# Half of an S5 layer's gate products moved from its output stage to its input stage

## The chip, the cores and the metric

The kernel runs on one core of a Trainium2 chip. The metric is the device time of one execution in microseconds (us). The engines of the core have one instruction queue each: TensorE (PE, matrix products; PEld is its weight load), VectorE (DVE), ScalarE (ACT), GpSimd (POOL) and SyncE (SP), which issues most of the DMAs. Before the change, three runs took 1774.8, 1778.39 and 1779.83 us.

## The reference, cut to what matters

The program is two layers of a network over 512 latent and 256 context tokens. The first layer is attention. The second, which the change is in, is a bidirectional S5 state-space layer with a gated output:

```python
u, g = split(h @ w_in, 2)              # 2048 channels each; g is used for the latent tokens only
for direction in (forward, backward):  # 128 groups of 16 channels, 64 complex states in each
    x[t] = lam_bar * x[t-1] + b_bar @ u[t]
    y += real(c @ x[t])
y = gelu(y + d * u)                    # tanh form
ya, yb = split(y @ w_glu + b_glu, 2)
out = ((ya * sigmoid(yb)) * silu(g)) @ w_out
```

The kernel treats eight tokens as one step of the recurrence, so that 512 tokens are 64 steps.

## The kernel before, in words

All large products are done as three PE passes over high and low halves (`mm3`, lines 81 to 83). A weight tile of 128x1024 is loaded by SP into `wraw` (2 buffers), ACT casts it to `whi` and DVE subtracts to get `wlo` (line 65; 3 buffers each). `wnext` (line 1023) keeps up to three such tiles ahead of their use; `wsrc` lists them in the order of use.

The S5 layer has these parts.

- **Input loop**, `for t in range(18)`. `u_tile(t)` makes 128 of the 2048 channels of u, for latent and context tokens (48 matmuls on PE), and stores them. `u_load(t-1)` reads them back in another layout. `s_tile(t-2)` makes from them what is added to the states (line 1134, a block of 32 matmuls), and ACT copies it to the state tiles `ST` (lines 1140 to 1143). After every second `s_tile`, `tree` (lines 1164 to 1169, DVE) folds the context tokens into the start state. After every fourth, a new recurrence begins: `rec.append(recur(...))`. There are four of them, each for 32 groups, of 63 steps each.
- **Recurrence.** One step is four small DVE instructions on 128x64 (lines 1179 to 1182), each but the second dependent on earlier ones. `pull(n)` writes n steps of every recurrence under way into the program. In the loop it stands in three or four places of an iteration (12 steps for t from 6 to 14). The scratch tiles `rt1`, `rt2` have two buffers, so at most two steps are under way.
- **Gates.** `gates` computes silu(g) for 128 channels and 512 tokens: 24 matmuls on PE, a tanh on ACT (line 1218), a multiply on DVE (line 1219), a store by SP (line 1220), then `pull(4)`. There are sixteen. All stand behind the input loop: seven ahead of the first output tile, nine between output tiles.
- **Output tiles**, m from 0 to 15. `y_load(m)` has SP load 512 KB twice (`wo`), 256 KB (`u`) and, for every second m, 1 MB (`toe`). `states(m)` has ACT copy the finished states of tile m (lines 1253, 1254); tiles 4q to 4q+3 need the whole of recurrence q. `y_tile(m)` is 48 matmuls on PE (line 1268) and a DVE copy. After m = 2, 3, 6, 7, 10, 11, 14, 15 `gelu` transposes two tiles on PE (line 1281) and runs for each a chain ACT, DVE, ACT, DVE, ACT, DVE (lines 1285 to 1288, 76, 77) through the scratch tile `t`.
- **GLU.** `glu_mm` is a unit of 24 matmuls against eight of the sixteen GELU outputs. The first eight units in `GLU_ORDER` need outputs 0 to 7 only (tiles 0 to 7). Four units stand between the output tiles, the rest behind them, then the output product.

The order between output tiles is a string; the letter g is a gate, a is a GLU unit:

```python
gates(6, gg)
states(0)
gates(1, gg)
...
        if "gggggggg.g.a.aaa"[m] == "g":
            gates(1, gg)
        elif "gggggggg.g.a.aaa"[m] == "a":
            glu_mm()
```

The order of the program is not yet the order on the chip. When the tile context closes, a planner runs through the program against its own cost model. When an engine is free in that model, it gives it the earliest instruction of the program whose inputs and buffers are ready then. The result is a fixed queue per engine, which the chip follows in order. So an instruction can be planned ahead of an earlier one that was still waiting in the model. Once it is in the queue, everything behind it on that engine waits for it.

Of the kernel before, what the change touches and what calls it, by code (L numbers as in the profile page):

```python
# [9 lines left out]
F32 = mybir.dt.float32  # L10
# [8 lines left out]
P = 128  # L19
# [12 lines left out]
def hybrid_mla_s5(ctx, tc, I, O):  # L32
# [895 lines left out]
    def two(i):  # L928
        return ps2[i % 2].tile([P, 2, 512], F32, name="mm2")
# [52 lines left out]
    def res_load(tt, n):  # L982

        c = slice(512 * n, 512 * n + 512)
        if (n, tt // 4) not in gates0:
            g = gates0[n, tt // 4] = xp.tile([P, 512], F32, name="g", bufs=2)
            sp.dma_start(out=g, in_=gtrow[0][tt // 4:tt // 4 + 1, c].broadcast_to([P, 512]))
        x = xp.tile([P, 512], F32, name="x")
        sp.dma_start(out=x, in_=I["xp"][tt * P:(tt + 1) * P, c])
        return x, gates0[n, tt // 4]  # L990
# [4 lines left out]
    for h in range(HEADS):  # L995
# [4 lines left out]
        if h < 9:  # L1000
            if 2 <= h < 8:
                tt = h - 2
                x, g = res_load(tt, 0)
# [11 lines left out]

    GLU_ORDER = [(m, k, h) for h in range(2) for m in range(4) for k in (1, 0)]
    GLU_ORDER += [(m, k, h) for m in range(4, 16) for k in (1, 0) for h in range(2)]
    wsrc = [I["win1"][m] for m in range(32)]
    wsrc += [I["wglu"][m, k][:, D * h:D * h + D] for m, k, h in GLU_ORDER]
    wsrc += [I["wout1"][m] for m in range(8)]  # L1020
    wq, wdma = [], [sp]
# [1 line left out]
    def wnext():  # L1023
        while wsrc and len(wq) < 3:
            raw = wp.tile([P, D], F32, name="wraw", bufs=2)
            wdma[0].dma_start(out=raw, in_=wsrc.pop(0))
            wh = wp.tile([P, D], F32R, name="whi")
            wl = wp.tile([P, D], F32R, name="wlo")
            split(wh, wl, raw)
            wq.append((wh, wl))  # L1030
        return wq.pop(0)

    def proj1(w, s):
        wh, wl = w
        o = bank()[:, :(TL, TC)[s]]
        for kc in range(KC):
            k = slice(kc * P, (kc + 1) * P)
            mm3(o, wh[:, k], wl[:, k], H1[s][:, 0, kc, :], H1[s][:, 1, kc, :], kc == 0, kc == KC - 1)
        return o
# [52 lines left out]
    def win_chunk(c):  # L1092
        pt = wins[c] = winp.tile([P, 4, 2, P], F32, name="pt", bufs=5)
        sp.dma_start(out=pt, in_=wid[c])
# [15 lines left out]
    def u_tile(m):  # L1110
        w = w_first.pop(0) if w_first else wnext()
        ol = o_first.pop(0) if o_first else proj1(w, 0)
        oc = proj1(w, 1)
        ub = up.tile([P, 8, 96], F32, name="ub", bufs=1)
        act.copy(ub[:, :, 0:64], ol.rearrange("p (i k) -> p i k", k=64))
        act.copy(ub[:, :, 64:96], oc.rearrange("p (i k) -> p i k", k=32))
        act.dma_start(out=ud[m].rearrange("i p k -> p i k"), in_=ub)
        act.dma_start(out=udl[m].rearrange("i p k -> p i k"), in_=ub[:, :, 0:64])

    def u_load(m):  # L1120
        us[m] = up.tile([P, 8, 96], F32, name="u", bufs=3)
        sp.dma_start(out=us[m], in_=ud[m].rearrange("i (c g) k -> (i c) (g k)", g=8))

    def s_tile(m):

        if m % 2 == 0:
            scs[m // 2] = up.tile([P, 2, 16, 32], F32, name="sc")
        sc = scs[m // 2]
        for c in (2 * m, 2 * m + 1):
            wi = wins.pop(c)  # L1130
            o = two(c)
            for q in range(4):
                for r in range(2):
                    pe.matmul(o[:, r, 96 * q:96 * (q + 1)], wi[:, q, r, :], us[m][:, 4 * (c % 2) + q, :],  # L1134
                              start=True, stop=True)
            o = o[:, :, :384].rearrange("p r (q k) -> p r q k", k=96)
            g = slice(4 * c % 32, 4 * c % 32 + 4)
            gc = slice(4 * c % 16, 4 * c % 16 + 4)
            st = ST[c // 8].rearrange("p k r g -> p r g k")
            act.copy(st[lo_, :, g, 1:64], o[lo_, :, :, 0:63])  # L1140
            act.copy(st[up_, :, g, 1:64], o[up_, :, :, 63:0:-1])
            act.copy(sc[lo_, :, gc, :], o[lo_, :, :, 64:96])
            act.copy(sc[up_, :, gc, :], o[up_, :, :, 95:63:-1])
# [10 lines left out]
    def tree(k):  # L1154

        x = scs.pop(k)
        gs = slice(16 * k, 16 * k + 16)
        for l in range(5):
            n = 16 >> l
            a = up.tile([P, 2, 16, n], F32, name=f"tr{l}", bufs=1)  # L1160
            b = up.tile([P, 2, 16, 16], F32, name="trb", bufs=1)[:, :, :, :n]
            lr, li = lam(l, gs, n)
            ev, od = x[:, :, :, 0::2], x[:, :, :, 1::2]
            dve.tensor_tensor(a, ev, lr, op=ALU.mult)
            dve.tensor_tensor(b, ev[:, ::-1], li, op=ALU.mult)
            dve.tensor_tensor(a, a, b, op=ALU.add)
            g = slice(16 * k % 32, 16 * k % 32 + 16)
            dst = a if l < 4 else ST[k // 2][:, 0, :, g].unsqueeze(3)
            dve.tensor_tensor(dst, a, od, op=ALU.add)
            x = a  # L1170

    def recur(q, work):

        st = ST[q]
        lr, li = lam(0, slice(32 * q, 32 * q + 32), 0)
        for k in range(63):
            t1 = work.tile([P, 2, 32], F32, name="rt1", bufs=2)
            t2 = work.tile([P, 2, 32], F32, name="rt2", bufs=2)
            dve.tensor_tensor(t1, st[:, k], lr, op=ALU.mult)
            dve.tensor_tensor(t2, st[:, k, ::-1, :], li, op=ALU.mult)  # L1180
            dve.tensor_tensor(st[:, k + 1], st[:, k + 1], t1, op=ALU.add)
            dve.tensor_tensor(st[:, k + 1], st[:, k + 1], t2, op=ALU.add)
            yield

    rec = []

    def pull(n):
        for _ in range(n):
            for r in list(rec):
                if next(r, 0) == 0:  # L1190
                    rec.remove(r)

    for c in range(2):
        win_chunk(c)
    for t in range(18):
        if 1 <= t <= 16:
            u_load(t - 1)
        if t < 16:
            u_tile(t)
            pull(3)  # L1200
        if t < 15:
            for c in (2 * t + 2, 2 * t + 3):
                win_chunk(c)
                pull(3)
        m = t - 2
        if m >= 0:
            s_tile(m)
            pull(3)
            if m % 2 == 1:
                tree(m // 2)  # L1210
            if m % 4 == 3:
                rec.append(recur(m // 4, stp))

    def gates(n, tile):
        for m in itertools.islice(todo, n):
            o = proj1(wnext(), 0)
            g = tile()[:, :TL]
            act.activation(g, o, AF.Tanh, scale=0.5)
            dve.scalar_tensor_tensor(g, g, 1.0, o, op0=ALU.add, op1=ALU.mult)
            sp.dma_start(out=gd[m], in_=g)  # L1220
            pull(4)
# [2 lines left out]

    def gg():
        return stp.tile([P, TL], F32, name="gg", bufs=2)

    ues.close()
    wines.close()
# [46 lines left out]
    def gelu(n):  # L1276

        o = two(0).rearrange("p a (j e k) -> p (a j) e k", e=2, k=64)
        src = ot.pop(n)
        for j in range(8):  # L1280
            pe.transpose(o[:, j], src[:, j].rearrange("p a x -> p (a x)"), ident)
        for e in range(2):
            y = o[:, :, e, :]
            t = ep.tile([P, 8, 64], F32, name="t", bufs=1)
            act.activation(t, y, AF.Square, scale=0.044715 ** 0.5)
            dve.scalar_tensor_tensor(t, t, 1.0, y, op0=ALU.add, op1=ALU.mult)
            act.activation(t, t, AF.Tanh, scale=0.7978845608028654)
            dve.scalar_tensor_tensor(t, t, 1.0, y, op0=ALU.add, op1=ALU.mult)
            v = 2 * n + e
            h, l = (VV[v // 4][:, v % 4, i] for i in range(2))  # L1290
            half_split(t, *(x.rearrange("p (j k) -> p j k", k=64) for x in (h, l)))
            V[v] = h, l
# [18 lines left out]
    y_load(1)  # L1311
    wdma[0] = sp

    gates(6, gg)
    states(0)
    gates(1, gg)
    for m in range(16):
        y_tile(m)
        if m + 2 < 16:
            y_load(m + 2)  # L1320
        pull(4)
        if m < 15:
            states(m + 1)
        if "gggggggg.g.a.aaa"[m] == "g":
            gates(1, gg)
        elif "gggggggg.g.a.aaa"[m] == "a":
            glu_mm()
        if m % 4 == 2:
            VV.append(stp.tile([P, 4, 2, TL], F32R, name="st"))
        if m % 4 >= 2:  # L1330
            gelu(m // 2 - (m % 2 == 0))
# [10 lines left out]
    while GLU_ORDER:  # L1342
        m, k, h = glu_mm()
        if (k, h) == (0, 1):
            g = work.tile([P, TL], F32, name="g")
            sp.dma_start(out=g, in_=gd[m])
            t = work.tile([P, TL], F32, name="t2")
# [10 lines left out]
    with mkpool(name="f_s", bufs=1, side="right") as work:  # L1358
# [34 lines left out]
        for tt in range(4):  # L1393
# [5 lines left out]
            for n in range(2):  # L1399
                c = slice(512 * n, 512 * n + 512)  # L1400
# [106 lines left out]
```

## Time and profile before

| what | value |
|---|---|
| runs | 1774.8, 1778.39, 1779.83 us |
| profiled execution | 1775.6 us |
| its span (first to last instruction) | 1773.8 us |
| granted TensorE clock, mean | 0.941 of full |
| PE busy | 1573.9 us (89%) |
| DVE busy | 948.8 us (53%) |
| ACT busy | 731.1 us (41%) |
| POOL busy | 657.7 us (37%) |

All times below are counted from the start of the span. Full TensorE clock is 2.4 GHz; a granted clock of 0.78 is the mean of a stretch in which the clock was partly at its lower level, 1.2 GHz. Busy times over the whole span say little here: the attention layer, the input loop, the output tiles and the GLU have different limits, so each stretch is read on its own. The input loop lies between about 960 and 1151 us, the output tiles between 1181 and 1336 us, the GLU and the output product behind them.

### The profile page before, as it was taken

Reading aid. Unit: us, or ns where it says so; the run is one execution under the profiler, and the core shown is the slowest. Engines: PE = TensorE matmul, PEld = TensorE weight load, DVE = VectorE, ACT = ScalarE, POOL = GpSimd, SP = SyncE. Lnnn points to the kernel's source line nnn. Section 1 sums busy time; section 2 is a strip of 40 time slices with the busy share of each in tenths; the row PEclk is TensorE's granted clock in tenths of the full one; section 3 lists DMA queues with packets and bytes.
Section 4 is the critical chain, followed back from the end, with each engine's and each line's share of the span. In section 5 each row is a group of like instructions: output and inputs, shape, how many; then the busy total and the mean of one; then the engine's idle time right before and its main releaser. Section 6 shows DMA issues by size and latency. Waiting matters only on the chain.

```text
span 1773.8 us, 26950 instructions
## 1 busy us (share of the span) xinstructions
PE 1573.9 (89%) x9870; PEld 1313.6 (74%) x9870; DVE 948.8 (53%) x2478; ACT 731.1 (41%) x1253; POOL 657.7 (37%) x705
## 2 busy tenths in 40 slices
PE   7548788999887977789999999999869999999997
PEld 4435467887786867678887999988658888888876
DVE  7352222376565755667435288899953433333336
ACT  2221122365545644556214666767473222222220
POOL 2999758899677878771000000000000000000022
PEclk9868798999989988989999999999889999999999
DMA  9216776564455565555424866578462333333442
GB/s 338 75 50 217 240 238 194 161 208 121 143 176 163 169 166 166 164 166 172 125 77 134 258 214 230 171 270 320 154 243 77 123 109 108 108 107 107 128 156 72
DMA packets 157132, 293.60 MB, mean 166 GB/s; under 512 B 55068, under 2 KB 86856, under 8 KB 155976
## 3 DMA queue, kind: packets, MB, share of 16 engines
q1 hardware_dynamic: 122056, 279.07, 48.6%
q10 hardware_dynamic: 34880, 12.78, 2.8%
q8 instruction: 78, 1.28, 0.3%
q14 instruction: 54, 0.44, 0.1%
q0 software_dynamic: 64, 0.03, 0.0%
HBM read 230.39 MB, written 69.55 MB: 169 GB/s over the span
## 4 chain that ended last, share of the span: by engine, by line
PE 53%; DMA 18%; POOL 16%; DVE 5%; issue 4%; ACT 3%; SPq 0%; ACTq 0%; POOLq 0%
PE mm L81 15%; PE mm L83 15%; PE mm L82 15%; DMA wo<-pind 8%; DMA wid<-wo 4%; PE mm L1134 3%; DMA pair<-in_w_mod_dram 2%; DMA wraw<-in_wout_dram 2%; POOL wo L395 1%; POOL pw L393 1%; PE mm L1268 1%; POOL wt L391 1%; POOL bk L361 1%; POOL wo L394 1%; POOL wt L390 1%
## 5 line engine op out<-in xcount | busy, mean ns | idle before, releaser
L65 DVE TENSOR_TENSOR wlo<-wraw,whi 128x1024 fp32r<-128x1024 f32 (+1 forms) x155 | 178.5, 1153 | 337.0 <-ACT whi L65 332.7
L1371 POOL TENSOR_TENSOR x<-x,row_g 128x1024 f32<-128x1024 f32 x4 | 11.3, 2846 | 926.0 <-DMA wraw<-in_wout_dram 886.6
L65 ACT CAST whi<-wraw 128x1024 fp32r<-128x1024 f32 (+1 forms) x155 | 149.4, 965 | 401.3 <-PE mm L82 268.2
L81 PE MATMUL mm<-st,whi 128*128 128x512 f32 x512 | 204.2, 399 | 5.2 <-ACT st L76 5.1
L83 PE MATMUL mm<-st,wlo 128*128 128x512 f32 x512 | 202.5, 396 | 0.0
L82 PE MATMUL mm<-st,whi 128*128 128x512 f32 x512 | 201.4, 393 | 0.8 <-DVE st L77 0.8
L81 PE MATMUL mm<-h,whi 128*128 128x512 f32 (+1 forms) x384 | 138.7, 362 | 0.2 <-DVE bnmv L917 0.2
L82 PE MATMUL mm<-h,whi 128*128 128x512 f32 (+1 forms) x384 | 137.1, 358 | 0.8 <-DVE h L1077 0.8
L83 PE MATMUL mm<-h,wlo 128*128 128x512 f32 (+1 forms) x384 | 136.5, 356 | 0.0
L81 PEld LDWEIGHTS mm<-st,whi 128*128 128x128 f32 x512 | 97.5, 190 | 26.8 <-ACT st L76 6.3
L81 PE MATMUL mm<-hh,whi 128*128 128x512 f32 (+1 forms) x320 | 112.2, 361 | 3.2 <-DVE hh L599 3.2
L82 PEld LDWEIGHTS mm<-st,whi 128*128 128x128 f32 x512 | 97.3, 190 | 23.3 <-DVE st L77 1.6
L83 PEld LDWEIGHTS mm<-st,wlo 128*128 128x128 f32 x512 | 97.4, 190 | 22.6
L83 PE MATMUL mm<-hh,wlo 128*128 128x512 f32 (+1 forms) x320 | 109.7, 346 | 1.1 <-DVE wlo L65 1.0
L82 PE MATMUL mm<-hl,whi 128*128 128x512 f32 (+1 forms) x320 | 110.4, 347 | 0.0
L65 DVE TENSOR_TENSOR ptl<-tr,pth 128x384 fp32r<-128x384 f32 (+1 forms) x160 | 79.0, 524 | 17.3 <-ACT pth L65 16.5
L65 ACT CAST pth<-tr 128x384 fp32r<-128x384 f32 (+1 forms) x160 | 68.5, 462 | 45.9 <-PE tr L832 45.3
L808 ACT ACTIVATE p<-sc,mx 128x768 f32<-128x768 f32 (+1 forms) x96 | 73.6, 766 | 27.9 <-DVE mx L807 27.6
L807 DVE TENSOR_REDUCE mx<-sc 128x1 f32<-128x768 f32 (+1 forms) x96 | 73.8, 772 | 17.4 <-PE sc L797 16.4
L81 PEld LDWEIGHTS mm<-h,whi 128*128 128x128 f32 x384 | 72.9, 190 | 12.0 <-issue 0.5
L82 PEld LDWEIGHTS mm<-h,whi 128*128 128x128 f32 x384 | 73.0, 190 | 10.8 <-DVE h L1077 1.1
L83 PEld LDWEIGHTS mm<-h,wlo 128*128 128x128 f32 x384 | 72.9, 190 | 10.4
(371 smaller groups left out, 4196.5 us busy)
## 6 DMA issues: line engine op xcount, KB each, us to landing
wraw<-in_wglu_dram SPq DMA_DIRECT2D x64, 512.0 KB
wraw<-in_win_dram SPq DMA_DIRECT2D x52, 512.0 KB
wod<-wo SPq DMA_DIRECT2D x32, 512.0 KB
wo<-pind SPq DMA_DIRECT2D x32, 512.0 KB
pw<-in_Bc_dram SPq DMA_DIRECT2D x32, 512.0 KB
wid<-wo SPq DMA_DIRECT2D x32, 512.0 KB
pt<-wid SPq DMA_DIRECT2D x32, 512.0 KB
wo<-wod SPq DMA_DIRECT2D x32, 512.0 KB
```

The costliest lines, as they stand in the source:

```text
L65: return act.copy(hi, src).ins, (eng or dve).tensor_tensor(lo, src, f(hi), op=ALU.subtract).ins
L81: pe.matmul(ps, lh, rh, start=first, stop=False)
L82: pe.matmul(ps, lh, rl, start=False, stop=False)
L83: pe.matmul(ps, ll, rh, start=False, stop=last)
L361: pool.tensor_tensor(bk[rows, :, :, 16 * d:16 * d + 16], b1[rows], b2[rows], op=ALU.add)
L390: eng.tensor_tensor(t1, pr, br, op=ALU.mult)
L391: eng.tensor_tensor(t2, pi, bi, op=ALU.mult)
L393: eng.tensor_tensor(bi, pr, bi, op=ALU.mult)
L394: eng.tensor_tensor(pr, t1, t2, op=ALU.add)
L807: dve.reduce_max(mx[:, 1:2], s, axis=AX.X, negate=True)
L808: act.activation(p[:, a:b], s, AF.Exp, bias=mx[:, 1:2], scale=1.0, accum_out=mx[:, 2:3])
L1134: pe.matmul(o[:, r, 96 * q:96 * (q + 1)], wi[:, q, r, :], us[m][:, 4 * (c % 2) + q, :], start=True, stop=True)
```

## The change

Eight of the sixteen gates are called inside the input loop, behind `u_tile(t)` for t = 4, 5, 7, 8, 10, 11, 13, 14, each with its `pull(4)`. One stays ahead of `states(0)` and one behind it. Six are left between the output tiles, behind m = 0, 2, 4, 6, 8 and 10. The GLU units keep their places. The weight list follows the new order. The scratch tile `t` of the GELU gets a second buffer. `gates`, `todo` and `gg` move up unchanged.

```diff
-    wsrc = [I["win1"][m] for m in range(32)]
+
+    GATE_AT = (4, 5, 7, 8, 10, 11, 13, 14)
+    wsrc = [I["win1"][m] for t in range(16) for m in (t,) + ((16 + GATE_AT.index(t),) if t in GATE_AT else ())]
+    wsrc += [I["win1"][m] for m in range(24, 32)]
...
         if t < 16:
             u_tile(t)
             pull(3)
+            if t in GATE_AT:
+                gates(1, gg)
...
-            t = ep.tile([P, 8, 64], F32, name="t", bufs=1)
+            t = ep.tile([P, 8, 64], F32, name="t", bufs=2)
...
-    gates(6, gg)
+    gates(1, gg)
     states(0)
     gates(1, gg)
...
-        if "gggggggg.g.a.aaa"[m] == "g":
+        if "g.g.g.g.g.ga.aaa"[m] == "g":
             gates(1, gg)
-        elif "gggggggg.g.a.aaa"[m] == "a":
+        elif "g.g.g.g.g.ga.aaa"[m] == "a":
             glu_mm()
```

## Rows read from the trace of the kernel before

**Rows 1.** Engines by stretch: length, busy us (instructions), granted clock, DMA share, GB/s.

```profile
1029.00:1160.00 131.00, 131.00 (x858) 119.27 (x857) 112.28 (x549) 89.94 (x127) 0.00 (x0) 1.00 0.60 198
1160.00:1257.00 97.00, 96.60 (x722) 80.32 (x721) 93.00 (x443) 62.71 (x60) 0.00 (x0) 1.00 0.85 310
1257.00:1280.00 23.00, 16.82 (x63) 11.92 (x63) 22.93 (x121) 7.08 (x11) 0.00 (x0) 0.78 0.35 114
1280.00:1336.00 56.00, 38.94 (x424) 33.05 (x422) 31.47 (x116) 42.69 (x32) 0.00 (x0) 0.85 0.53 193
1360.00:1700.00 340.00, 339.75 (x1485) 278.61 (x1485) 112.45 (x111) 85.03 (x96) 9.80 (x4) 1.00 0.36 117
```

**Rows 2.** Line 1179 alone, by stretch: one instruction is one step of a recurrence.

```profile
1029.00:1160.00 131.00, 23.87 (x108) 1.00 0.60 198
1160.00:1257.00 97.00, 20.62 (x94) 1.00 0.85 310
1257.00:1279.30 22.30, 5.58 (x26) 0.77 0.36 118
1279.30:1315.00 35.70, 5.38 (x24) 0.81 0.59 221
```

**Rows 3.** ACT in order of time: start, us; the copies that wait for a recurrence.

```profile
1279.28 2.07 ACT L1253 COPY sm<-st 64x1024 f32<-64x1024 f32 x1 [4.92 <-DVE st L1182]
...
1314.84 2.08 ACT L1253 COPY sm<-st 64x1024 f32<-64x1024 f32 x1 [1.69 <-DVE st L1182]
```

**Rows 4.** PE in order of time: two matmuls of consecutive gates, 24 matmuls apart.

```profile
1160.08 0.39 PE L82 MATMUL mm<-h,whi 128*128 128x512 f32 x1
...
1165.52 0.39 PE L82 MATMUL mm<-h,whi 128*128 128x512 f32 x1
```

**Rows 5.** Groups of DVE instructions, 1029.2 to 1314.8: busy us, mean ns, idle before.

```profile
L65 DVE TENSOR_TENSOR wlo<-wraw,whi 128x1024 fp32r<-128x1024 f32 x27 | 32.9, 1219 | 6.8 <-ACT whi L65 6.6
...
L1219 DVE SCALAR_TENSOR_TENSOR gg<-gg,mm 128x512 f32<-128x512 f32 x16 | 10.9, 680 | 0.5 <-ACT gg L1218 0.5
```

**Rows 6.** DVE in order of time: starts of steps, one recurrence, then a pair.

```profile
1079.00 0.22 DVE L1179 TENSOR_TENSOR rt<-st,lamt 128x64 f32<-128x64 f32 x1
1079.80 0.22 DVE L1179 TENSOR_TENSOR rt<-st,lamt 128x64 f32<-128x64 f32 x1
...
1087.26 0.23 DVE L1179 TENSOR_TENSOR rt<-st,lamt 128x64 f32<-128x64 f32 x1
...
1088.35 0.22 DVE L1179 TENSOR_TENSOR rt<-st,lamt 128x64 f32<-128x64 f32 x1
```

**Rows 7.** Waits of DVE: us, times, longest; in the loop, then from 1160 to 1315.

```profile
DVE tr L1164 <- ACT sc L1143: 13.7, 6, 3.0
...
DVE st L77 <- ACT st L76: 2.1, 1, 2.1
```

**Rows 8.** SP's own waits, 960 to 1340 us.

```profile
SPq L1094 <- PE mm L1134: 90.8, 20, 8.7
...
SPq L1220 <- DVE rt L1180: 2.5, 4, 0.9
```

**Rows 9.** Chain that ended last: one output tile on PE, one GELU's transposes.

```profile
1189.99 2.77 PE mm L1268 x48
...
1206.86 0.87 PE mm L1281 x8
```

**Rows 10.** Groups of PE instructions, 1257 to 1336: output tiles, GLU units, transposes.

```profile
L1268 PE MATMUL mm<-wo,sm 128*64 128x128 f32 x256 | 22.2, 301 | 7.9 <-ACT sm L1254 7.9
L1268 PE MATMUL mm<-toe,u 128*64 128x128 f32 x120 | 13.5, 306 | 9.1 <-DMA u<-udl 8.8 <-DVE st L1181 0.3
L82 PE MATMUL mm<-st,whi 128*128 128x512 f32 x24 | 12.0, 499 | 0.8 <-DVE st L77 0.8
...
L1281 PE MATMUL mm<-ident,ot 128*128 128x128 f32 x32 | 4.8, 300 | 0.4 <-DVE st L1182 0.4
```

**Rows 11.** DMA rate while output tiles are loaded fastest (columns as in Rows 1).

```profile
1180.00:1200.00 20.00, 19.60 (x179) 16.29 (x179) 18.34 (x99) 13.02 (x10) 0.00 (x0) 1.00 1.02 401
```

More of the change, by code (lines that the diff above doesn't have):

```diff
@@ L1191, in pull, with gates, gg @@
                     rec.remove(r)
+    def gates(n, tile):
+        for m in itertools.islice(todo, n):
+            o = proj1(wnext(), 0)
+            g = tile()[:, :TL]
+            act.activation(g, o, AF.Tanh, scale=0.5)
+            dve.scalar_tensor_tensor(g, g, 1.0, o, op0=ALU.add, op1=ALU.mult)
+            sp.dma_start(out=gd[m], in_=g)
+            pull(4)
+    todo = iter(range(16))
+    def gg():
+        return stp.tile([P, TL], F32, name="gg", bufs=2)
     for c in range(2):
@@ L1212, in hybrid_mla_s5 @@
                 rec.append(recur(m // 4, stp))
[L1214 to L1221, printed above, removed]
-    todo = iter(range(16))
-    def gg():
-        return stp.tile([P, TL], F32, name="gg", bufs=2)
     ues.close()
```

## The prediction

> **What bounds the kernel now.** The busy times by stretch come first, because the change lies between 960 and 1336 us only. In the input loop PE is busy for all of its 131 us at full clock; DVE is busy for 112.3 of them [rows 1]. From 1160 to 1257 both are nearly full. From 1257 to 1336 PE falls behind: it is busy 55.8 of 79 us at a granted clock of 0.78 and 0.85. From 1360 on it is full again, so what is lost before 1336 reaches the end one for one.
>
> What does PE wait for there? The count of steps answers. Of 252 steps 108 are done by 1160, 94 follow by 1257, 26 by 1279, 24 by 1315 [rows 2]. The program places 150 in the input loop (12 per iteration from t = 6 to 14, then 6, 3 and 3 for what is under way). So DVE is some 40 steps behind when the loop ends. ACT copies the states of tile 8 at 1279.28 and those of tile 12 at 1314.84, each time as soon as the recurrence lets it [rows 3]. These are the ends of the third and the fourth recurrence; tiles 8 to 11 and 12 to 15 follow them.
>
> So the gates that the change moves are PE work in a stretch where PE has no gap, and they go to one where it has none either. The eight gates cost 8 x 5.44 = 43.5 us of PE there [rows 4], and the same is taken away behind. PE runs out of other work at about 1257 in both versions, if nothing else intervenes. What decides is when the recurrences end, and what PE has to do meanwhile.
>
> PE's loss now: in 1257 to 1336 it does 72 GLU matmuls at 5.44/24 us (16.3; three units), 376 matmuls of output tiles, 2.77 us for 48 (21.7), and 32 transposes at 0.87 for 8 (3.5) [rows 4, 9, 10]. That is 41.5 us of work in 79 us: 23.2 idle and 14.3 to the lower clock.
>
> **The change part by part.**
>
> *Start of the first recurrence.* It needs the states of `s_tile(3)`, in iteration 5. Two gates now stand ahead of it, at t = 4 and 5, on a PE that has no gap: +10.9 us. DVE has no steps to do in that time, since none is ready. The bounds are 0 (the planner puts these gates behind) and 10.9; I take 10.9, as a ready gate is earlier in the program.
>
> *DVE work done before that start.* Each gate takes a `wlo` of 1.22 and a multiply of 0.68 on DVE [rows 5]. Two gates' worth leaves the later queue: -3.8. The other six are on DVE between the first and the last step before and after: 0.
>
> *Fewer pairs.* A lone recurrence takes 0.79 us a step, two together 1.09 for two steps [rows 6], so a pair saves 0.49. By counting pulls, the old program has 15 pairs of the first two recurrences, 15 of the next two and 39 of the last two: 69. The new one pulls 16 in an iteration with a gate, ends recurrences earlier against the next one's start, and has 7 + 3 + 35 = 45. The 24 lost pairs cost 24 x 0.49 = 11.8 if nothing else fills the gaps of a lone chain, and 0 if tree and split instructions fill all. In the loop they alternate with the steps about half of the time; I take 5.
>
> *Idle DVE in the longer loop.* DVE idles 131 - 112.3 = 18.7 us of the loop, 14%, of which 13.7 stand in front of a tree head that waits for ACT [rows 1, 7], with steps queued behind it. Six gates behind the start lengthen the stretch by 32.6 us; at 14% that is +4.7. The far end is that the longer loop lets the steps into the idle time: -18.7, the third rival. I take the row's own share.
>
> *Second scratch tile.* The two chains of one GELU may now overlap. DVE waited 2.1 us on this chain between 1160 and 1315 [rows 7], so -2.1 at most for the steps queued behind it, which I take; PE's own waits for these outputs fall into the wait for the third recurrence, which covers them. Without that cover the tile would be worth what PE waits for line 77 there, 0.8 us [rows 10], and a little more.
>
> *Stores and waits.* Eight gate stores move on SP ahead of loads for the loop. In the rows such a store waits 0.9 us at longest, while the loop's own loads wait 8.7 for PE to free a buffer [rows 8]; 8 x 0.9 = 7.2 is the far end, 0 the value, the cover being those waits. Behind a store stand the `pt` and `u` loads and the next weight tile. The tanh stands in ACT's queue ahead of the state copies; ACT is busy 89.9 of 131 us [rows 1], so a gate's cast and tanh fit into its 5.44 us. The far end is a further tree head per gate pushed back, already in the idle share.
>
> *Tile loads.* A tile loads 1.84 MB (512 KB twice, 256 KB, and half of 1 MB), a gate 0.52 MB of weights and 0.26 MB stored. Before, a tile with its gate and half a GELU takes 2.77 + 5.44 + 0.44 = 8.65 us of PE for 2.62 MB, 303 GB/s. Now every second of tiles 0 to 7 has a gate: 5.93 us for 2.23 MB, 376 GB/s. The fastest stretch shows 401 GB/s [rows 11], so it just fits: 0. If only 303 to 310 were kept up, a tile would take 7.3 us: 8 x 1.4 = +11 on PE. The Trainium skill, page "Perfetto Trace Analysis", section "Roofline", puts the ceiling of a single core at about 435 GB/s, set by its 16 DMA engines; no run here shows that rate. By it a tile would need 5.1 us, and by the row 5.6; either is under 5.93, and by the page alone the second rival would have less than the chance that I give it.
>
> *Sum for the recurrences.* 10.9 - 3.8 + 5 + 4.7 - 2.1 = +14.7: the fourth ends at about 1329 in place of 1314.8, the third ends 28 lone steps ahead of it in place of 24, which at 35.7/24 us each [rows 2] is 1288.
>
> *What of it reaches PE.* Tiles 12 to 15 follow as before, so the output stage ends 14.7 later. Against that, PE can put GLU units into the longer wait. Eight need only tiles 0 to 7; three were done by 1336, five are left (27 us). Bounds 0 and -14.7. The old order took a unit only where no output tile was ready, and each needs its `wlo` from the same full DVE. I take one unit, -5.4. That leaves +9.3.
>
> 1775.6 + 9.3 = 1784.9 us for an execution like the profiled one, which lies 2.8 under the median of the three runs; against that median it would be 1787.7. I say 1786.
>
> **The rivals.**
>
> *Second: the loads hold the tiles and nothing fills the wait.* Tiles 0 to 7 come late at 376 GB/s, so do their GELUs, and the GLU units can't start while PE waits. Then 14.7 stays whole, and the clock falls with the longer gaps: 14.3 us were lost beside 23.2 idle, so 0.62 x 14.7 = 9.1 more. 1775.6 + 23.8 = 1799.4. For it: the demand is 94% of the best rate shown. Against: the gates can run ahead of the tiles and space them out.
>
> *Third, the other side: the longer loop empties DVE's backlog.* At tree heads DVE stands still with steps in its queue. If the planner puts the steps pulled behind the gates ahead of these heads, the idle 18.7 us are used: 10.9 - 3.8 + 5 - 2.1 - 18.7 = -8.7, or 1766.9; with another GLU unit in a gap 1761.5. It decides from 10.0 of the 18.7 us on. For it: a backlog of 40 steps at the loop's end. Against: the queue is fixed, and before there was as much to place and the gaps stayed.
>
> *Fourth: no net change.* PE has the same work and five GLU units to hide behind: if it takes three in place of one, 9.3 falls to -1.6 or so and the time is 1774 to 1779. The same would show if the planner left the gates where they ran before; with PE full in the loop and the gates ready, little speaks for that.
>
> **How the numbers follow.** Chances: forecast (+2 to +16) 0.42, second 0.14, third 0.27, fourth 0.17. Differences under 0.3%, 5.3 us, can't be told from none. Slower takes 0.35 of the forecast and the second, 0.49. Same takes 0.07 of the forecast and 0.16 of the fourth, 0.23. Faster takes the third and 0.01 of the fourth, 0.28. The forecast's own range is 1778 to 1794. The whole range goes from 1764, under the third case, to 1804, the second case on the median's basis (1802.2) and a little: about 0.1 is left out on each side.
>
> **What would show it.** The first step starts at about 1040 in place of 1029, PE stays full to the end of the loop, and fewer than 154 steps are done when it ends. ACT's first copy for tile 8 comes near 1288 and for tile 12 near 1329, each released by line 1182. DVE's idle time in the loop is 22 us or more. From about 1257 PE waits with a granted clock under 1. I am wrong if the fourth recurrence ends at 1315 or before, if PE has more than four GLU units done when tile 15 is, or if the first recurrence starts as early as before.

## The result and the profile after

The changed kernel takes 1800.4 us (median of four runs, 1794.0 to 1804.5). The kernel before takes 1778.9 beside it. The ratio is 1.0121, with a 95% interval from 1.0095 to 1.0147: slower by 21.5 us. The prediction said 1786, slower, with a range from 1764 to 1804. The profiled span is 1799.1 us, 25.3 more than before. One execution further below stands apart, the profiled one of e5: it took 2218.7 us at a granted clock of 0.648, so it is left out and no row of e5 is read.

The busy times of the changed kernel by stretch, with the columns of [rows 1]:

```profile
960.00:1197.70 237.70, 237.70 (x1487) 213.75 (x1485) 161.56 (x680) 137.20 (x194) 0.00 (x0) 1.00 0.65 205
1197.70:1217.00 19.30, 0.13 (x3) 0.16 (x4) 18.29 (x92) 11.47 (x9) 0.00 (x0) 0.57 0.61 215
1217.00:1303.00 86.00, 79.17 (x620) 65.99 (x620) 77.35 (x370) 49.80 (x50) 0.00 (x0) 0.92 0.72 259
1303.00:1362.00 59.00, 38.46 (x416) 33.72 (x418) 35.26 (x135) 42.19 (x32) 0.00 (x0) 0.80 0.52 183
1362.00:1725.00 363.00, 363.00 (x1598) 298.04 (x1594) 123.93 (x126) 94.25 (x108) 9.48 (x4) 1.00 0.35 115
```

PE is full up to the end of the input loop, now at 1197.7, and full again from 1362 on. Between them lie two stretches of loss. One was there before, at the end of the output tiles. The other is new: 19 us at the loop's end in which PE does nothing. The one PE row that shows it, in order of time:

```profile
1216.88 0.70 PE L1273 MATMUL mm<-toe,u 128*64 128x128 f32 x4 [19.17 <-DMA u<-udl]
```

The steps of the recurrences by stretch (line 1182 in this kernel; compare [rows 2]):

```profile
1029.00:1160.00 131.00, 21.54 (x96) 1.00 0.64 203
1160.00:1257.00 97.00, 19.18 (x86) 0.88 0.66 234
1257.00:1303.00 46.00, 9.54 (x42) 0.91 0.61 212
1303.00:1343.00 40.00, 6.28 (x28) 0.79 0.57 210
```

By 1160 there are 96 steps done (108 before), by 1257 there are 182 (202 before). The ACT copies that need the third and the fourth recurrence, which [rows 3] has at 1279.28 and 1314.84, come 23.8 and 28.2 us later:

```profile
1303.05 2.03 ACT L1258 COPY sm<-st 64x1024 f32<-64x1024 f32 x1
...
1343.03 2.00 ACT L1258 COPY sm<-st 64x1024 f32<-64x1024 f32 x1 [1.69 <-DVE st L1185]
```

The output tiles end at 1362.4 (1336 before, +26.4), and the rest of the program follows at full clock. So the time is lost before 1362, and the question is what on DVE made the fourth recurrence 28 us late. Its groups of instructions between the first step and tile 12's copy (1040.2 to 1343) are: busy us, mean ns, idle time before them.

```profile
L1182 DVE TENSOR_TENSOR rt<-st,lamt 128x64 f32<-128x64 f32 x252 | 56.5, 224 | 4.3
...
L1185 DVE TENSOR_TENSOR st<-st,rt 128x64 f32<-128x64 f32 x252 | 53.5, 225 | 4.3
...
L65 DVE TENSOR_TENSOR wlo<-wraw,whi 128x1024 fp32r<-128x1024 f32 x26 | 31.8, 1224 | 7.5 <-ACT whi L65 7.4
...
L1201 DVE SCALAR_TENSOR_TENSOR gg<-gg,mm 128x512 f32<-128x512 f32 x14 | 9.6, 684 | 0.0
L1276 DVE COPY ot<-mm 128x512 f32<-128x512 f32 x12 | 8.3, 688 | 3.8 <-PE mm L1273 3.7
...
L1293 DVE SCALAR_TENSOR_TENSOR t<-t,mm 128x512 f32<-128x512 f32 x12 | 8.2, 686 | 3.2 <-ACT t L1292 3.1
```

In the kernel before, the same groups between its first step and its tile 12 (1029.2 to 1314.8) that [rows 5] does not show:

```profile
L1179 DVE TENSOR_TENSOR rt<-st,lamt 128x64 f32<-128x64 f32 x252 | 55.4, 220 | 2.9
...
L1182 DVE TENSOR_TENSOR st<-st,rt 128x64 f32<-128x64 f32 x252 | 50.6, 220 | 2.5
...
L1271 DVE COPY ot<-mm 128x512 f32<-128x512 f32 x12 | 8.2, 685 | 0.7 <-PE mm L1268 0.7
...
L1288 DVE SCALAR_TENSOR_TENSOR t<-t,mm 128x512 f32<-128x512 f32 x12 | 8.2, 683 | 0.1
```

The instructions of a step overlap within a line and between lines, so the busy times of the lines don't add up to time on DVE. The step instructions, as the only ones that use the scratch tiles `rt`, can be taken together, and beside them everything on DVE (the third busy time, as in [rows 1]); before, then after:

```profile
1029.20:1314.80 285.60, 164.70 (x1008) 0.96 0.66 233
1040.20:1343.00 302.80, 173.90 (x1008) 0.92 0.64 216
...
1029.20:1314.80 285.60, 266.85 (x1862) 230.12 (x1861) 255.25 (x1219) 183.65 (x215) 0.00 (x0) 0.96 0.66 233
1040.20:1343.00 302.80, 262.49 (x1826) 228.72 (x1824) 261.83 (x1216) 179.78 (x212) 0.00 (x0) 0.92 0.64 216
```

The same 1008 step instructions take 173.9 us in place of 164.7. Counted in the traces in order of time, two recurrences take a step side by side 69 times before and 45 times after, just as the prediction had counted from the pulls. So 24 pairs less go with 9.2 us more, 0.38 each. Idle time grows too, at the output copies (0.7 to 3.8) and in the GELU chain (0.1 to 3.2): these instructions stand in DVE's fixed queue with steps behind them. Over the whole stretch DVE is busy 261.8 us in place of 255.3 and idle 41.0 in place of 30.3. With the later start (1040.2 in place of 1029.2) that is 11.0 + 6.5 + 10.7 = 28.2.

### The profile page after: what moved, and what is told of

The parts are those of the page before. It is cut to its first block, busy times and chain, and to the rows that moved or that the text cites. A ratio compares the mean times of both kernels' runs of the same rounds, so it can differ in the third digit from the quotient of the medians.

```text
span 1799.1 us, 26939 instructions
## 1 busy us (share of the span) xinstructions
PE 1576.0 (88%) x9870; PEld 1319.0 (73%) x9870; DVE 962.2 (53%) x2478; ACT 730.3 (41%) x1253; POOL 659.3 (37%) x705
## 4 chain that ended last, share of the span: by engine, by line
PE 52%; DMA 18%; POOL 16%; DVE 5%; issue 4%; ACT 4%; SPq 1%; ACTq 0%; POOLq 0%; DVEq 0%
PE mm L81 15%; PE mm L82 15%; PE mm L83 15%; DMA wo<-pind 7%; DMA wid<-wo 3%; PE mm L1137 3%; DMA pair<-in_w_mod_dram 2%; DMA wraw<-in_wout_dram 2%; PE mm L1273 1%; POOL wo L394 1%; POOL wo L395 1%; POOL pw L393 1%; POOL wt L390 1%; POOL wt L391 1%; ACT sm L1259 1%
```

## The experiments

Theory A is the prediction's: the fourth recurrence's end sets the end of the output tiles. Theory B is the new hole of 19 us. The table has where the last instruction of each run's last step begins, when ACT copies for tile 12, and the ratio to the kernel before.

| kernel | last step instruction, us | tile 12's copy | span | ratio (95%) |
|---|---|---|---|---|
| before | 1314.6 | 1314.8 | 1773.8 | 1 |
| after | 1342.8 | 1343.0 | 1799.1 | 1.0121 (1.0095 to 1.0147) |
| e1, hole filled | 1345.7 | 1347.3 | 1803.6 | 1.0157 (1.0135 to 1.0179) |
| e2, gates late | 1337.3 | 1337.6 | 1794.1 | 1.0121 (1.0100 to 1.0142) |
| e3, two early gates | 1325.4 | 1326.0 | 1784.5 | 1.0039 (1.0024 to 1.0053) |
| e4, one scratch tile | 1339.1 | 1339.4 | 1798.4 | 1.0113 (1.0092 to 1.0134) |
| e10, no pulls in the loop | 1330.6 | 1330.8 | 1787.8 | 1.0082 (1.0060 to 1.0105) |
| e12, e2 and e10 together | 1319.3 | 1323.9 | 1780.9 | 1.0058 (1.0040 to 1.0075) |
| e11, less on DVE, gates as before | 1307.9 | 1308.5 | 1770.8 | 0.9975 (0.9959 to 0.9991) |

**e1, the hole filled.**

```diff
-    gates(1, gg)
+    gates(6, gg)
...
-        if "g.g.g.g.g.ga.aaa"[m] == "g":
+        if "g..........a.aaa"[m] == "g":
```

> The changed kernel, but with its eight remaining gates arranged as six ahead of the first state copy, one behind it and one behind output tile 0, so that seven stand ahead of the first output tile as before the change. Theory A (the fourth recurrence ends late and sets the end of the output tiles): the 19.2 us in which PE stands idle ahead of the first output tile go away, but the fourth recurrence still ends at 1338 to 1345 us and the time stays at 1796 to 1802 us; PE's idle time comes back ahead of tile 8. Theory B (that idle stretch of 19.2 us is what the change costs): the time falls by 15 to 19 us, to 1781 to 1785 us.

PE is busy for all of 1197.7 to 1217, so the hole is gone, and the time is 1805.6, not less (3.6 above theory A's range). The fourth recurrence ended at 1346, its copy followed at 1347, and PE waited for it there. Theory B as the cost by itself falls: PE had only moved its waiting.

**e2, the gates later in the loop; e3, only two early gates; e4, one scratch tile.** e2:

```diff
-    GATE_AT = (4, 5, 7, 8, 10, 11, 13, 14)
+    GATE_AT = (7, 8, 10, 11, 12, 13, 14, 15)
```

> The changed kernel with its eight loop gates at t = 7, 8, 10, 11, 12, 13, 14, 15, so that none stands ahead of the first recurrence. Theory A: the first step starts at 1029 in place of 1040 us, the fourth recurrence ends 8 to 11 us earlier (1332 to 1335), and the time is 1789 to 1792 us. Theory B: the two gates ahead of the first output tile are as many as before, so the idle stretch and the time stay: 1799 to 1801 us.

e3, against the kernel before (which keeps its string of gates):

```diff
+    GATE_AT = (4, 5)
...
+            if t in GATE_AT:
+                gates(1, gg)
...
-    gates(6, gg)
+    gates(4, gg)
```

> The kernel before with only two gates moved, to t = 4 and 5 (four are left ahead of the first state copy, one scratch tile for the GELU, the order between output tiles as before). Theory A: the first step starts at 1040 us, the fourth recurrence ends 7 to 11 us later (1322 to 1326) and the time is 1786 to 1790 us against 1779. Theory B: with five gates ahead of the first output tile PE has next to no idle stretch there: 1779 to 1782 us.

e4:

```diff
-            t = ep.tile([P, 8, 64], F32, name="t", bufs=2)
+            t = ep.tile([P, 8, 64], F32, name="t", bufs=1)
```

> The changed kernel with one scratch tile for the GELU. Theory A as predicted: the second tile is worth 2 us to the steps queued behind, so 1800 to 1803 us. Theory B: nothing, 1799 to 1801 us. A third view, that two overlapping GELU chains push the steps of the recurrence back in VectorE's queue, gives less than 1797 us.

e3 came as theory A has it: 1785.7 us, tile 12's copy 11.2 later. But in e2, where the first step is back at 1029.2, the copy is only 5.4 earlier than in the changed kernel, the span 5.0 less, and the ratio is the same: 1798.9 us against an expected 1789 to 1792, a miss. The step instructions of e2 and all of its DVE from its first step to tile 12's copy:

```profile
1029.20:1337.60 308.40, 175.82 (x1008) 0.94 0.64 216
...
1029.20:1337.60 308.40, 268.71 (x1874) 233.82 (x1872) 266.62 (x1220) 184.24 (x218) 0.00 (x0) 0.94 0.64 216
```

Of the 11.0 us of earlier start 4.8 go to more busy time than in the changed kernel and 0.8 to more idle time. Two gates' work on DVE stands behind the first step again, and only 39 pairs are left in e2's trace, six fewer than in the changed kernel. So the late start is a real cost, but moving the gates late brings other costs back. e4 (1797.5 us, in none of its three ranges) shows no difference from the changed kernel by its interval; the second scratch tile is worth nothing that can be told.

**e5 and e6, half the steps in every recurrence.** For e5 in the kernel before and for e6 in the changed one:

```diff
-        for k in range(63):
+        for k in range(31):
```

> The kernel before, with every recurrence doing 31 of its 63 steps (the other 32 are left out, so the states behind them are not the reference's). Theory A (the late end of the fourth recurrence sets the end of the output tiles): 128 steps less, some 100 us of DVE, so no recurrence ends last any more; PE's loss between 1257 and 1336 (23.2 us idle and 14.3 from the lower clock) goes: 1738 to 1748 us. Rival C (loads of the output tiles and weight tiles set the pace there, the recurrences only stand beside them): 1760 to 1776, with PE's waits for y tiles put down to DMA.

> The changed kernel with the same 31 steps in every recurrence. Theory A: what the change cost through the recurrences (tile 12's copy 28 us later) is gone; only the wait of 19.2 us ahead of the first output tile, which the recurrences covered, can show now: 1740 to 1765, at most 20 above the shortened kernel before, and after that wait PE has no idle above 5 us before tile 15. Rival C (the loads of the moved gates and of the closer output tiles cost the time): some 21 us or more above the shortened kernel before, spread over the output tiles, PE's waits put down to wo, u or toe.

e5 took 1748.5 to 1754.3 us, ratio 0.9845 (0.9809 to 0.9881). That lies between theory A's range and rival C's. e6 took 1774.5, ratio 0.9971 (0.9953 to 0.9989). Between them lies 0.9971 / 0.9845 = 1.0128, as much as the change costs with full recurrences. Theory A allowed 20 us for the uncovered hole; 21 to 22 came, which is rival C's number. The waits are not spread over loads as rival C has it, though. PE's waits in e6 from 1190 to 1345 (us, times, longest):

```profile
PE mm L1273 <- DMA u<-udl: 17.2, 2, 16.9
PE mm L1286 <- DVE t L1293: 10.6, 5, 2.9
```

No line of a recurrence is in it. So with the recurrences out of the way there is a second limit, by which the change costs as much as by the first: the hole, and waits on the GELU chain behind it.

**e7 and e8, the low halves of the weights on POOL.** For the kernel before (e7) and the changed one (e8):

```diff
             wl = wp.tile([P, D], F32R, name="wlo")
-            split(wh, wl, raw)
+            split(wh, wl, raw, pool)
```

> The kernel before, with the low halves of the S5 layer's weight tiles computed on POOL, which is idle there, in place of DVE. Theory A: the recurrences lose 27 instructions of 1.22 us and 6.8 us of waits for them from DVE's queue (39.7 us); the fourth ends at 1275 to 1295 in place of 1314.8 and PE's loss shrinks as much: 1745 to 1765 us. Rival D: a 128x1024 on POOL takes some 2.8 us (its adds of that size in the last stage) and DVE's small instructions get slower beside it, so weights come later to PE and the recurrences gain under 10 us: 1770 to 1790.

> The changed kernel with the same low halves on POOL. Theory A: 26 instructions of 1.22 us and 7.5 us of waits (39 us) leave DVE's queue, the fourth recurrence ends at 1300 to 1320 in place of 1343.0: 1762 to 1782 us, still above the kernel before with POOL, by 10 to 22, since the recurrences still start 11 us later and are alone more often. If the change's loss were in PE's or the loads' part, the two POOL versions would differ by the same 21 us or more and the wait ahead of the first output tile would set it. Rival D: 1790 to 1810.

e7 took 1798.7 us, ratio 1.0111 (1.0081 to 1.0141): rival D's direction, and past its range. e8 took 1816.2, ratio 1.0212 (1.0177 to 1.0247), past rival D's range too. DVE has 27 instructions less in e7 and its recurrences still end 8 us later than before. Its rows in order of time, POOL and DVE together, show why:

```profile
1040.83 2.45 POOL L65 TENSOR_TENSOR wlo<-wraw,whi 128x1024 fp32r<-128x1024 f32 x1 [9.59 <-ACT whi L65]
1040.83 0.23 DVE L1182 TENSOR_TENSOR st<-st,rt 128x64 f32<-128x64 f32 x1
1041.09 2.26 DVE L1179 TENSOR_TENSOR rt<-st,lamt 128x64 f32<-128x64 f32 x1
1043.28 0.21 DVE L1180 TENSOR_TENSOR rt<-st,lamt 128x64 f32<-128x64 f32 x1
```

A DVE instruction of 0.22 us that comes up while POOL works lasts 2.26 us, until POOL is done. So 1.22 us of DVE's own work was exchanged for some 2.1 us of standing still. More is lost than the recurrences show: e7's output tiles end at 1355.6, 19.5 us late, with PE waiting 11.6 and 9.7 us for DVE ahead of two blocks of transposes, and later 5.1 us for one `wlo` from POOL. The two runs differ by 17.5 us, within theory A's 10 to 22. But since DVE was slowed in both, and neither recurrence ended where theory A had it, the pair does not tell the theories apart.

**e9, the hole filled and half the steps.** The edits of e1 and e6 together:

> The changed kernel with seven gates ahead of the first output tile (none behind tiles 1 to 10 but the one at m = 0), and 31 of 63 steps in every recurrence (the other 32 left out). Theory E (two limits of about the same size, one behind the other: the recurrences end 28 us later, and PE has a hole of 17 to 19 us with waits on the GELU chains behind it; taking away one leaves the other): with both taken away the time is that of the shortened kernel before, 1753 us: 1748 to 1760. Theory A alone would have had the shortened changed kernel there already. Rival C (the moved gates' loads and stores cost the time wherever the gaps are): 1768 us or more, as with the hole.

1774.6 us, ratio 0.9984 (0.9968 to 0.9999), the same as e6: theory E in its simple form, that the hole is the second limit, falls, and rival C's number came. e9 by stretch:

```profile
1198.00:1227.60 29.60, 29.60 (x134) 24.25 (x132) 24.17 (x92) 19.48 (x20) 0.00 (x0) 1.00 0.73 253
1227.60:1260.00 32.40, 24.03 (x277) 20.53 (x277) 26.50 (x104) 24.14 (x19) 0.00 (x0) 0.89 0.96 363
1260.00:1300.00 40.00, 29.07 (x287) 22.35 (x285) 14.64 (x22) 30.56 (x27) 0.00 (x0) 0.82 0.73 260
1300.00:1337.00 37.00, 34.94 (x362) 28.53 (x360) 16.47 (x23) 31.27 (x28) 0.00 (x0) 0.96 0.60 208
```

With the gates spent ahead of the first tile, the tiles and GELUs behind it have no PE work beside them, and PE, bare of gates, loses what the hole had cost. PE's largest wait from 1190 to 1345, and its only one for a load:

```profile
PE mm L81 <- ACT st L76: 17.8, 4, 7.1
...
PE mm L1273 <- DMA wo<-wod: 0.2, 1, 0.2
```

The first is GLU units that wait for a GELU output. So the second limit is the pace of the output stage behind a loop that ends 44 us later (its last s_tile ends at 1195.4 in the changed kernel, 1151.6 before), not the hole as such. For 32 us the DMA engines are nearly full (0.96), but PE hardly waits for them, and of the chain that ended last there one weight tile's load (6.0 us at 1231) is the longest on DMA. So rival C's number came, and its cause is not seen. The trace points at ACT: from 1227.6 to 1337 it is busy 86.0 of 109.4 us, and in that chain the GELU's activations stand behind the copies of `states`, here behind four of them (8.3 us):

```profile
1239.00 2.04 ACT sm L1258
1241.05 2.07 ACT sm L1259
1243.14 2.08 ACT sm L1258
1245.22 2.05 ACT sm L1259
1247.30 0.61 ACT t L1290
```

No run takes these copies off ACT, so this is read from the trace and not shown by an experiment.

**e10, no steps written behind the gates in the loop.**

```diff
-            pull(4)
+            pull(0 if t < 17 else 4)
```

> The changed kernel with no steps written behind the eight gates in the input loop, so that it has the pulls of the kernel before there, and 69 pairs in place of 45. Pair theory (lone steps cost DVE the 7 us more that its step instructions are busy in the changed kernel): step instructions busy 211 to 214 us in place of 218, the fourth recurrence ends 4 to 8 us before 1343, time 1791 to 1797. Rival F (a later place in the program only delays steps, since DVE takes what is ready): the fourth recurrence at 1345 or later, 1800 us or more.

1790.1 us, just under the range. The two lines of a step in e10 that have idle time in front of them, from 1042 to 1331, then its step instructions together and all of its DVE:

```profile
L1182 DVE TENSOR_TENSOR rt<-st,lamt 128x64 f32<-128x64 f32 x252 | 55.8, 222 | 2.7
...
L1185 DVE TENSOR_TENSOR st<-st,rt 128x64 f32<-128x64 f32 x252 | 50.9, 222 | 2.8
...
1042.30:1330.80 288.50, 165.48 (x1008) 0.96 0.66 226
...
1042.30:1330.80 288.50, 254.59 (x1826) 222.03 (x1824) 253.43 (x1217) 179.57 (x212) 0.00 (x0) 0.96 0.66 226
```

The trace has 69 pairs again. The step instructions take 165.5 us, close to the 164.7 before the change, with 5.5 us of idle time in front of them in place of 8.6. The recurrences end 12.2 us earlier (4 to 8 expected): DVE is busy 8.4 us less, which is what the pairs give back (173.9 to 165.5), and idle 5.9 us less, with a first step 2.2 us later. So the pair theory holds for the busy time. That the idle time shrinks as well was not in it, and no run parts the two. Steps that the change put into the program earlier made the end later.

**e12, late gates without pulls.** The edits of e2 and e10 together:

> The changed kernel with its eight gates in the input loop from t = 7 on (so that the first recurrence starts at 1029 again) and no steps written behind them (so that the 69 pairs are back): the two terms of the recurrence path that the runs so far showed one by one (5.4 and 12.2 us at the end of the fourth) are both taken away. If they add, the fourth recurrence ends at 1323 to 1328 (1343.0 in the changed kernel, 1314.8 before) and the time is 1781 to 1788 us. What is left over the kernel before then belongs to neither: the fourth recurrence starts 43 us later, behind a longer loop, and the output stage has the hole ahead of its first tile. If the rest were nothing, the time would be 1779 or less; if the two terms were one and the same, 1789 or more.

1787.5 us, and 1780.9 in the profiled span. The last step's last instruction begins at 1319.3, 23.5 us before that of the changed kernel, and 4.7 behind the kernel before. That is more than the 17.6 of the two terms: with 68 pairs in its trace, e12 also gets back those that e2 had lost. Together the two edits give back most of the 28.2 us. But tile 12's copy does not follow at once, as e12's ACT shows in order of time:

```profile
1322.39 1.04 ACT L65 CAST whi<-wraw 128x1024 fp32r<-128x1024 f32 x1 [3.96 <-PE mm L82]
1323.35 0.62 ACT L1292 ACTIVATE t<-t 128x512 f32<-128x512 f32 x1
1323.88 2.01 ACT L1258 COPY sm<-st 64x1024 f32<-64x1024 f32 x1
```

A weight cast waits 4 us for PE to free its buffer, and the copy is queued behind it. Of the 21.5 us some 11 went (1800.4 - 1787.5 = 12.9 by the medians, 0.0063 of 1778 = 11.2 by the ratios); 10 stay with the recurrences almost back in place. In the profiled execution 7.1 us of span stay, and tile 12's copy is 9.1 late: 4.7 by the recurrence and 4.4 in ACT's queue. The hole is still there too (18.0 us). Whether this is the limit of e6 and e9 is not shown.

**e11, less on DVE, the gates as before.** Against the kernel before:

```diff
+            act.copy(sc[lo_, :, gc, :], o[lo_, :, :, 64:96])
+            act.copy(sc[up_, :, gc, :], o[up_, :, :, 95:63:-1])
             act.copy(st[lo_, :, g, 1:64], o[lo_, :, :, 0:63])
             act.copy(st[up_, :, g, 1:64], o[up_, :, :, 63:0:-1])
-            act.copy(sc[lo_, :, gc, :], o[lo_, :, :, 64:96])
-            act.copy(sc[up_, :, gc, :], o[up_, :, :, 95:63:-1])
...
-        dve.tensor_copy(ot[m // 2]...
+        act.copy(ot[m // 2]...
```

> The kernel before, with less on DVE's way to the ends of the recurrences and no POOL: the copies of the output tiles out of PSUM go from DVE to ACT (12 of 0.685 us before the fourth recurrence ends), and in s_tile ACT does the sc copies ahead of the st copies, so that the tree heads (13.7 us of DVE idle) wait up to two copies of 1.09 us less each. Theory A: the fourth recurrence ends 10 to 22 us before 1314.8 and the time falls with it: 1756 to 1768 us. Rival: ACT is late instead (state copies behind the output copies, casts behind the sc copies) and PE waits for it: 1772 us or more.

1772.0 us, ratio 0.9975 (0.9959 to 0.9991): the one version with all steps that is faster than both kernels, by 4 to 5 us over the kernel before, where 10 to 22 were expected. The rival's bound, 1772 or more, is just met. The two groups of DVE in e11 that tell most, from 1029 to 1308:

```profile
L65 DVE TENSOR_TENSOR wlo<-wraw,whi 128x1024 fp32r<-128x1024 f32 x28 | 34.2, 1222 | 11.4 <-ACT whi L65 11.3
...
L1164 DVE TENSOR_TENSOR tr<-sc,lamt 128x512 f32<-128x512 f32 x6 | 4.1, 691 | 8.1 <-ACT sc L1141 8.1
```

The tree heads wait 8.1 us, 5.6 less [rows 7]. But ACT now casts later, and DVE waits 11.4 for `whi` where it waited 6.8 [rows 5]. The recurrences end 6.3 us earlier for 8.2 us of copies removed, and PE still waits 8.2 us for loads of u, as it did [rows 10].

## Why the prediction was right in sign and short in size

*What bounds the kernel.* Right for these two kernels: PE full in the loop and from 1362 on, the fourth recurrence's end in between. In the runs of the table with a later copy for tile 12 the span goes with it nearly one for one: 28.2 later gives 25.3, 11.2 gives 10.7, 16.0 (e10) gives 14.0. An earlier one gives less (6.3 gives 3.0 in e11). But the forecast had this limit alone. With half of the steps left out the change costs as much (e6), so a second limit lies right behind the first.

*Start of the first recurrence, +10.9.* The first step came 11.0 later. Taken back in the changed order, with the work that this puts behind the start, it gives 5.4 (e2); put into the kernel before, it costs all of it (11.2 in e3).

*DVE work before the start, -3.8.* The two groups lost 1.1 and 1.3 us, 2.4 in all.

*Fewer pairs, +5.* The pairs were counted rightly (69 and 45 in the traces) and mis-sized: the step instructions take 9.2 us more, near the far end of the bounds (11.8). The assumption that trees and splits fill half of a lone chain's gaps was wrong.

*Idle DVE in the longer loop, +4.7, and the second tile, -2.1.* The step that failed most. Together +2.6 was said; idle time grew by 10.7, and these 8.1 us are more than half of the 13.5 by which the sum falls short. It is not where it was sought: the tree heads wait 14.6 us in place of 13.7. It stands in front of the steps themselves (5.4 to 8.6 us over the two lines that have any) and of output instructions with steps behind them (two groups, together 6.2 more). In e10, with the pulls behind the gates left out, 5.9 of the 10.7 go. The second tile gave nothing (e4), and its chain waited more.

*Stores and tile loads, 0.* SP's waits at the gate stores are 1.1 us at longest, so these cost nothing that shows. The loads were not free: PE waited 27.0 us on u, 19.2 of it the hole, which the prediction did not see at all; the other 7.8 are no more than the 8.8 before [rows 10]. It counted the gates' PE work as moved, not that only two gates were left to cover the first loads, of which SP issues the first two `wo` at 1209, behind the loop:

```profile
1204.17 0.38 SPq L1244 DMA_DIRECT2D toe<-toed  x1
1209.29 0.80 SPq L1247 DMA_DIRECT2D wo<-wod  x2
```

Also, 376 GB/s was said to fit under 401; the changed kernel moved 259 from 1217 to 1303 and did not come to that demand, and e9's stretch with the DMA engines at 0.96 moved 363. The Trainium skill, page "Perfetto Trace Analysis", section "Roofline", would leave room up to about 435 GB/s; no stretch of a few tens of us here shows it.

*What reaches PE, -5.4.* PE had three GLU units done before tile 15, as before: nothing was absorbed. The delay of 28.2 at tile 12 became 26.4 at tile 15.

*Sum.* Said 14.7 for the recurrences, measured 28.2; said 9.3 at the end, measured 25.3 in the span and 21.5 in the medians. 1800.4 lies above the forecast's own range (1778 to 1794). It lies within the whole range only because of that range's upper end, which came from the second rival.

*Rivals.* The second named 1799.4, and its waits are there (no filling, a granted clock of 0.80 from 1303 to 1362), but its cause, output tiles held by their loads, can be seen in the hole alone. e1 shows that the hole does not set the end, and in e9 PE waits 0.2 us for a load. That its 1799.4 is near the result is luck. The third is refuted: 127 steps were done at the loop's end against 154 named, and DVE idled 23.6 us in it, above the 22 named. The fourth did not happen.

What stays open: of the second limit, the share of the hole, of the GELU chain and of ACT's queue; and why DVE's idle time grew by as much as it did.

## What to carry to other kernels

Moving filler work ahead can cost twice where a serial chain and its cover meet: here the chain started later, and the stage behind had less beside it to fill its waits. When one of two nearly equal limits is taken away and the time stays, take both away before judging either (e1, e6, e9). Where two latency-bound chains share an engine, count how many of their steps run side by side, in every variant (69, 45, 39 and 69 in before, after, e2 and e10); running one earlier and alone can make the end later.

## What was not expected of the hardware

POOL and DVE exclude each other here rather than share: a DVE tensor_tensor of 0.22 us lasted 2.26 beside a POOL one of 2.45 us. Each of the 27 POOL instructions in e7's stretch held one DVE instruction in this way, for 1.40 to 2.59 us. POOL's own 128x1024 took 2.46 us in the median and once 10.07 beside a DVE that had no pause (minimum/median/maximum in ns, first and last start):

```profile
L65 POOL TENSOR_TENSOR wlo<-wraw,whi x27: 2349/2456/10069, 1028.9 to 1333.3; 128x1024 fp32r<-128x1024 f32 x27
```

The Trainium skill, page "Trainium Architecture — The Big Picture", section "What this means for kernel authors", calls the port pair that the two share an exclusive lock and not a split of bandwidth; the rows agree.
